# One-core transformer stack: forgetting attention with shared row terms, two banks per step and divided probabilities

## Chip, core and metric

The kernel runs on one core of one Trainium2 chip. The metric is the device time of one execution in microseconds (us). PE is TensorE's matmul row, PEld its weight loads, DVE is VectorE, ACT is ScalarE, POOL is GpSimd.

## Reference, cut to what matters

Three layers run over 256 tokens of width 1024. The change lies in the third, in one of its three mixers, "forgetting attention" (fox): eight heads of width 64, softmax over earlier tokens, with a bias made of summed log gates.

```python
def _fox_mixer(q, k, v, f_logit, f_bias, q_g, k_g):
    ...
    log_f = jax.nn.log_sigmoid(f_logit.astype(jnp.float32) + f_bias.astype(jnp.float32))
    Fc = jnp.cumsum(log_f, axis=1).transpose(0, 2, 1)
    ...
    for blk in range(T // Q_BLOCK):                       # Q_BLOCK = 128
        lo, hi = blk * Q_BLOCK, (blk + 1) * Q_BLOCK
        s = (jnp.einsum('bhqd,bhkd->bhqk', qh[:, :, lo:hi], kh[:, :, :hi]) * scale
             + Fc[:, :, lo:hi, None] - Fc[:, :, None, :hi])
        mask = (lo + jnp.arange(Q_BLOCK))[:, None] >= jnp.arange(hi)[None, :]
        p = jax.nn.softmax(jnp.where(mask, s, -jnp.inf), axis=-1)
        outs.append(jnp.einsum('bhqk,bhkd->bhqd', p, vh[:, :, :hi]))
```

The term of the query's own row, `Fc[t]`, is the same for a whole row of the softmax and drops out; the kernel adds only the row `-Fc[s]`.

## The kernel before

The program writes TensorE's work in one stream. Projections (`prod`, lines 238 to 242, and `project_T`, lines 303 to 305) are the main stream; they multiply split float32r operands, with weights that arrive by DMA as `raw` and are split by ACT (`hi`, line 209) and DVE (`lo`, line 210). Norms and attention are side chains: generators that put their own products between those of the projections and yield an estimate of the microseconds that the other engines need before the chain goes on. A scheduler then orders each engine's instructions; each engine runs its own list in that order.

`fox(h)` is such a chain, for half h of the tokens (128 queries; h = 0 sees 128 keys, h = 1 sees 256). It is run for h = 0 and then for h = 1, woven into the projections of the values (line 1512) and of the first gate. `scores(q)` fills one PSUM bank: four heads for h = 0, two for h = 1. Per head it adds the row of summed gates (two products of an 8-row one-hot column with the rows' high and low parts `fs`, line 1278), the product of queries and keys (a float32 product of 64 rows, line 1284, recorded at the helper's line 363), and the mask (line 1288). Then come the negated maximum (DVE, line 1291) and an exponential per head with its sum (ACT, line 1294). `values` transposes the probabilities (line 329), copies them to SBUF (DVE, line 1302), and multiplies them, as the stationary operand of 128x128, with the values of 64 columns (line 1305, recorded at 363). At the end one DVE product divides all heads by their sums (line 1322), and four more transposes and `fill` make the split operand `yb` of the branch's projection, which comes much later in the stream.

Stick-breaking attention of the second layer (line 961 on) has products of the same forms elsewhere in this kernel: `zbanks` puts 64-row products of even and odd heads into two banks by turns, and its last loop holds the values stationary (64 columns) and writes heads to the lower and upper 64 partitions of one bank.

Of the kernel before, what the change touches and what calls it, by code (L numbers as in the profile page):

```python
# [13 lines left out]
P = 128  # L14
# [38 lines left out]
class Net:  # L53
    """Two halves of 128 tokens run skewed through the whole chain (nothing in the first half
    depends on the second), so that one half's products cover the other's dependent steps.
    Every projection holds the transposed activations stationary and streams the weights; both
    operands are split exactly into a float32r part and the float32r remainder, and three
    products carry each term.

    The program is traced in the order of the tensor engine's work: `steps` are the projections;  # L60
    norms and attention are side chains (generators that yield the microseconds their other
    engines need before the tensor engine's next part), woven in between a projection's products.
    """

    LEAD = 14.85  # how far ahead of its use a weight chunk is split
    LEAD_DMA = 24.0
    WARM = 5, 3, 2  # products of zeros in the gaps before the first projection

    def __init__(self, tc, ins, out, ctx, stop=99):
# [12 lines left out]
        self.now = 0.0  # the tensor engine's clock, by the count of its work  # L82
        self.main = 0.0  # the projections' share of it
# [3 lines left out]
        self.wplan = []  # (time of use, weight piece)  # L87
        self.plan = 0.0

# [33 lines left out]
    def get(self, slot):  # L123
        """waits for a slot in the projections' stream."""
# [32 lines left out]
    def weight(self, ap, r0, nk, c0, ncol, us=None):  # L157
        """plans a weight chunk for the steps planned next; its k tiles appear in ["hl"]."""
# [54 lines left out]
    def fetch(self, out, ap, late=False):  # L213
        """late: not ahead of the loads that are traced before."""
# [1184 lines left out]
    def second(self, x, xT, mk, mv, nxt):  # L1399
# [60 lines left out]
        def use_d(h, i, ps, r):  # L1460
            if i == 0:
                fsp[h] = self.fox_gate(ps[:, :8], r)
                if h == 1:
                    self.spawn(self.fox_rows(fsp, sl["fr"]))
# [256 lines left out]
```

## Time and profile before

| what | value |
|---|---|
| median of 3 runs | 1351.44 us (1350.68 to 1352.32) |
| span of the profiled execution, first to last instruction | 1349.8 us |
| PE busy | 1331.2 us (99%) |
| PEld busy | 1195.6 us (89%) |
| DVE busy | 811.7 us (60%) |
| ACT busy | 693.2 us (51%) |
| DMA read from HBM | 222.03 MB, 165 GB/s over the span |
| mean granted clock of TensorE | 0.992 |

The profiled execution's span is 1.6 us under the median; what lies around it (start and end of the program) is in the runs' times alone. PE's row counts a matmul until its modelled end, and consecutive matmuls overlap, so the time that a product really takes of the stream is the distance from its start to the next one's. A granted clock of 1.00 is 2.4 GHz, 0.50 is 1.2 GHz.

### The profile page before, as it was taken

The numbers are of one execution on the slowest core, as the hardware profiler recorded it, in microseconds if no ns is written. First come the engines' busy times: TensorE is split into PE (matmuls) and PEld (weight loads), VectorE is DVE, ScalarE is ACT, GpSimd is POOL, SyncE is SP. The second block draws the span as 40 slices with busy tenths as digits, with TensorE's granted clock in tenths as the row PEclk, the third lists the DMA queues.
The fourth block names the chain that finished last, engine by engine and source line by source line (L and its number), as shares of the span: only waits on it lengthen the run. The fifth ranks groups of instructions, "written<-read, shape, count | busy, mean of one in ns | idle before, by whom it ended". The sixth has DMA issues, their size and how long they took to land.

```text
span 1349.8 us, 21557 instructions
## 1 busy us (share of the span) xinstructions
PE 1331.2 (99%) x8506; PEld 1195.6 (89%) x8509; DVE 811.7 (60%) x1208; ACT 693.2 (51%) x1128; POOL 126.9 (9%) x224
## 2 busy tenths in 40 slices
PE   8999999999999999999999999998999999999998
PEld 5899888899998999888889999897987999899997
DVE  6665576644447565477664444767774456766552
ACT  6855555643437576574564344754443344645441
POOL 3000001000001000017100000114142020000000
PEclk9999999999999999999999999999997999999999
DMA  7854553646554643464464655463352346465551
GB/s 244 296 183 138 173 190 102 219 160 203 187 187 160 222 136 120 140 229 123 148 200 161 204 185 188 142 192 112 96 155 82 107 127 216 142 203 174 188 183 34
DMA packets 121439, 224.48 MB, mean 166 GB/s; under 512 B 7448, under 2 KB 19066, under 8 KB 121338
## 3 DMA queue, kind: packets, MB, share of 16 engines
q1 hardware_dynamic: 121338, 223.11, 51.5%
q8 instruction: 67, 1.10, 0.3%
q14 instruction: 34, 0.28, 0.1%
HBM read 222.03 MB, written 1.05 MB: 165 GB/s over the span
## 4 chain that ended last, share of the span: by engine, by line
PE 88%; DVE 4%; issue 3%; POOL 3%; ACT 2%; DMA 0%; DVEq 0%; ACTq 0%; POOLq 0%
PE mm L242 12%; PE mm L239 12%; PE mm L238 12%; PE tr L305 8%; PE tr L304 8%; PE tr L303 8%; PE tr L363 5%; PE mm L303 5%; PE mm L304 5%; PE mm L305 5%; PE tr L329 3%; PE tr L242 1%; PE tr L239 1%; PE tr L238 1%; DVE lo L210 1%
## 5 line engine op out<-in xcount | busy, mean ns | idle before, releaser
L210 DVE TENSOR_TENSOR lo<-raw,hi 128x1024 fp32r<-128x1024 f32 (+1 forms) x414 | 496.9, 1224 | 268.6 <-ACT hi L209 262.1
L209 ACT CAST hi<-raw 128x1024 fp32r<-128x1024 f32 (+1 forms) x414 | 419.7, 1042 | 221.2 <-PE mm L242 98.4
L238 PE MATMUL mm<-hi,t 128*128 128x512 f32 (+2 forms) x856 | 330.7, 388 | 0.0
L239 PE MATMUL mm<-lo,t 128*128 128x512 f32 (+2 forms) x856 | 328.4, 385 | 0.3 <-DVE lo L210 0.3
L242 PE MATMUL mm<-hi,t 128*128 128x512 f32 (+2 forms) x856 | 268.0, 388 | 0.0
L303 PE MATMUL tr<-t,hi 128*128 128x256 f32 x864 | 244.7, 283 | 0.0
L305 PE MATMUL tr<-t,lo 128*128 128x256 f32 x864 | 244.5, 283 | 0.0
L304 PE MATMUL tr<-t,hi 128*128 128x256 f32 x864 | 244.5, 283 | 0.0
L239 PEld LDWEIGHTS mm<-lo,t 128*128 128x128 f32 x856 | 162.1, 189 | 30.7 <-DVE lo L210 0.7
L238 PEld LDWEIGHTS mm<-hi,t 128*128 128x128 f32 x856 | 162.1, 189 | 29.0
L242 PEld LDWEIGHTS mm<-hi,t 128*128 128x128 f32 x856 | 159.7, 189 | 30.7 <-issue 0.4
L303 PE MATMUL mm<-t,hi 128*128 128x256 f32 x576 | 166.8, 290 | 0.0
L304 PEld LDWEIGHTS tr<-t,hi 128*128 128x128 f32 x864 | 165.8, 192 | 0.6
L303 PEld LDWEIGHTS tr<-t,hi 128*128 128x128 f32 x864 | 165.8, 192 | 0.6
L305 PEld LDWEIGHTS tr<-t,lo 128*128 128x128 f32 x864 | 165.8, 192 | 0.0
L305 PE MATMUL mm<-t,lo 128*128 128x256 f32 x576 | 163.7, 284 | 0.0
L304 PE MATMUL mm<-t,hi 128*128 128x256 f32 x576 | 163.7, 284 | 0.0
L303 PEld LDWEIGHTS mm<-t,hi 128*128 128x128 f32 x576 | 111.0, 193 | 1.6 <-issue 0.3
L304 PEld LDWEIGHTS mm<-t,hi 128*128 128x128 f32 x576 | 111.0, 193 | 0.8
L305 PEld LDWEIGHTS mm<-t,lo 128*128 128x128 f32 x576 | 110.9, 192 | 0.0
L375 POOL TENSOR_SCALAR s<-s 128x1 f32<-128x1 f32 x32 | 23.2, 725 | 798.0 <-ACT junk L381 786.8
L363 PE MATMUL tr<-t,t 128*128 128x128 f32 (+4 forms) x672 | 89.7, 297 | 4.1 <-DVE t L1155 3.4
(240 smaller groups left out, 1218.0 us busy)
## 6 DMA issues: line engine op xcount, KB each, us to landing
raw<-in_ffn_w_gate_up SPq DMA_DIRECT2D x88, 512.0 KB
raw<-in_ffn_w_down SPq DMA_DIRECT2D x66, 512.0 KB
raw<-in_w_in SPq DMA_DIRECT2D x54, 512.0 KB
raw<-in_ffn_w_up SPq DMA_DIRECT2D x44, 512.0 KB
raw<-in_xa_w_kv SPq DMA_DIRECT2D x32, 512.0 KB
raw<-in_sb_w_qkv SPq DMA_DIRECT2D x24, 512.0 KB
raw<-in_ml_w_in SPq DMA_DIRECT2D x22, 512.0 KB
raw<-in_xa_w_q SPq DMA_DIRECT2D x16, 512.0 KB
```

The costliest lines, as they stand in the source:

```text
L209: self.nc.scalar.copy(hi, raw)
L210: self.nc.vector.tensor_sub(lo, raw, hi.bitcast(F32))
L238: nc.tensor.matmul(out, lhsT=a, rhs=wh, start=first and k == 0, stop=False)
L239: nc.tensor.matmul(out, lhsT=a, rhs=wl, start=False, stop=False)
L242: nc.tensor.matmul(out, lhsT=b, rhs=hl[k][0], start=False, stop=last and k == nk - 1)
L303: self.nc.tensor.matmul(out, lhsT=wh, rhs=xh, start=k == 0, stop=False)
L304: self.nc.tensor.matmul(out, lhsT=wh, rhs=xl, start=False, stop=False)
L305: self.nc.tensor.matmul(out, lhsT=wl, rhs=xh, start=False, stop=k == kt - 1)
L329: self.nc.tensor.transpose(ps[:, i * P : (i + 1) * P], src(i), self.ident)
L363: self.nc.tensor.matmul(out, lhsT=lhsT, rhs=rhs, start=start, stop=stop, **kw)
L375: nc.gpsimd.tensor_scalar(e, a, EPS, b, ALU.add, ALU.add)
```

## The change

The row of summed gates becomes one product per head with 128 rows: the gates' sums are kept in one tile `f` of 128 partitions, the high part on rows 0 to 7 and the remainder on rows 32 to 39, zeros elsewhere, and `sel` selects both of a head's rows. A call of `scores` fills two banks, even heads in one and odd heads in the other: first one mask product for all heads of a bank, then the row terms, then the query-key products, which alternate between the banks. Sums are inverted per bank and each head's probabilities are divided on DVE before they are transposed. The values are the stationary operand (64 columns), the transposed probabilities stream (128 columns), and even and odd heads write the lower and the upper 64 partitions of `o`, which is then already the transposed result: the closing product and the closing transposes go. Yields in the chain are 6.0 and 2.4 where they were 1.5, 1.4 and 1.0.

```diff
-    def fox_gate(self, ps, r):
+    def fox_gate(self, ps, r, sp):
...
-        nc.vector.tensor_add(sp, a, e)
-        return sp
+        for c in (0, 32):
+            nc.vector.tensor_add(sp[:, c : c + 8], a, e)
...
-        mm(ps[:8, 0:128], lhsT=sp[0], rhs=self.up, start=True, stop=True)
-        mm(ps[:8, 128:256], lhsT=sp[1], rhs=self.up, start=True, stop=False)
-        mm(ps[:8, 128:256], lhsT=sp[0], rhs=self.onesf, start=False, stop=True)
-        fh, fl = self.t2([8, 256], F32R), self.t2([8, 256], F32R)
-        nc.vector.tensor_copy(fh, ps[:8, :256])
-        nc.vector.tensor_sub(fl, ps[:8, :256], fh.bitcast(F32))
-        slot.v = (fh, fl)
+        mm(ps[:, 0:128], lhsT=sp[:, 0, :], rhs=self.up, start=True, stop=True)
+        mm(ps[:, 128:256], lhsT=sp[:, 1, :], rhs=self.up, start=True, stop=False)
+        mm(ps[:, 128:256], lhsT=sp[:, 0, :], rhs=self.onesf, start=False, stop=True)
+        f = self.t2([P, 256], F32R)
+        nc.vector.tensor_copy(f, ps[:, :256])
+        nc.vector.tensor_sub(f[32:40], ps[32:40, :256], f[32:40].bitcast(F32))
+        slot.v = f
...
-        # even and odd heads in banks of their own
-        def scores(q):
...
+        def scores(g):
+            banks = [self.bank(), self.bank()]
+            vs = [b.rearrange("p (k s) -> p k s", k=per) for b in banks]
+            for v in vs:
+                nc.tensor.matmul(
+                    v[:, :, h * P :], lhsT=self.identb, rhs=self.m_nat[:, :per, :], start=True, stop=False, **kw
+                )
+            self.pe(MM * per / 2)
+            for i in range(per):
+                for q in range(2):
+                    hd = 2 * per * g + 2 * i + q
+                    nc.tensor.matmul(
+                        vs[q][:, i, :], lhsT=self.sel[:, hd : hd + 1].to_broadcast([P, P]), rhs=fr[:, : n * P],
+                        start=False, stop=False, **kw,
+                    )
+                    self.pe(MM * n / 4)
+            for i in range(per):
+                k = per * g + i
                 for s in range(n):
-                    self.mmf(
-                        v[:, i, s * P : s * P + P], sl["fq", h].v[r, hd // 2, :], sl["fk", s].v[r, hd // 2, :],
-                        False, s < h, **kw,
+                    for q in range(2):
+                        r = slice(q * 64, q * 64 + 64)
+                        self.mmf(
+                            vs[q][:, i, s * P : s * P + P], sl["fq", h].v[r, k, :], sl["fk", s].v[r, k, :],
+                            False, True, **kw,
+                        )
+            res = []
+            for v in vs:
+                mx, sm, rc = [self.small(per) for _ in range(3)]
+                nc.vector.tensor_reduce(mx, v, axis=AX.X, op=ALU.max, negate=True)
+                p = self.t2([P, per, n * P])
+                for i in range(per):
+                    nc.scalar.activation(
+                        p[:, i, :], v[:, i, :], AF.Exp, bias=mx[:, i : i + 1], accum_out=sm[:, i : i + 1]
+                    )
+                nc.vector.reciprocal(rc, sm)
+                for i in range(per):
+                    nc.vector.tensor_scalar(p[:, i, :], p[:, i, :], rc[:, i : i + 1], None, ALU.mult)
+                res.append(p)
+            return res
...
+            yield 2.4
+            for i in range(per):
+                k = per * g + i
                 for s in range(n):
-                    self.mmf(
-                        o[:, hd * 64 : hd * 64 + 64], pT[:, i, s, :], sl["fv", s].v[:, hd * 64 : hd * 64 + 64],
-                        s == 0, s == n - 1,
-                    )
+                    for q in range(2):
+                        hd = 2 * k + q
+                        self.mmf(
+                            o[q * 64 : q * 64 + 64, k * P : k * P + P], sl["fv", s].v[:, hd * 64 : hd * 64 + 64],
+                            pT[q][:, i, s, :], s == 0, s == n - 1, **kw,
+                        )
...
-        nc.vector.reciprocal(rc, sm)
-        t = self.t2()
-        nc.vector.tensor_mul(
-            t.rearrange("p (k t) -> p k t", k=8), o.rearrange("p (k t) -> p k t", k=8),
-            rc.unsqueeze(2).to_broadcast([P, 8, 64]),
-        )
-        yield 1.0
-        self.fill(self.transpose4(lambda i: t[:, i * P : (i + 1) * P]), y, h)
+        self.fill(o, y, h)
...
-        self.id8 = self.const([8, 8], F32R, "id8")
-        nc.vector.tensor_copy(self.id8, self.ident[:8, :8])
+        self.sel = self.const([P, 8], F32R, "sel")
+        nc.vector.tensor_add(self.sel, self.ident[:, 0:8], self.ident[:, 32:40])
+        self.fsp = self.const([P, 2, P], F32, "fsp")
+        nc.vector.memset(self.fsp, 0.0)
```

The order of instructions shows how the scheduler places this. First PE, at the first scores of half 0 in the program before: `tr_10614` is the bank of the scores, `t_9430` and `t_9431` the rows' high and low parts, `t_10569` and `t_10416` queries and keys.

```order
L1278 MATMUL tr_10614<-t_9430,id_5901 128x128
L1278 MATMUL tr_10614<-t_9431,id_5901 128x128
L363 MATMUL tr_10614<-t_10569,t_10416 128x128
L1288 LDWEIGHTS identb
L1288 MATMUL tr_10614<-m_nat,identb 128x128
L1278 MATMUL tr_10614<-t_9430,id_5901 128x128
```

The same place on PE in the changed program; two banks, `tr_10612` and `tr_10613`, and one tile of row terms, `t_9432`.

```order
L1277 LDWEIGHTS identb
L1277 MATMUL tr_10612<-m_nat,identb 128x512
L1277 LDWEIGHTS identb
L1277 MATMUL tr_10613<-m_nat,identb 128x512
L1284 MATMUL tr_10612<-t_9432,sel 128x128
L1284 MATMUL tr_10613<-t_9432,sel 128x128
...
L363 MATMUL tr_10612<-t_10570,t_10417 128x128
L363 MATMUL tr_10613<-t_10570,t_10417 128x128
```

Before, each head's three kinds of product follow one another, eight times in two blocks with six projection products between the blocks; now two masks, eight row terms and eight query-key products stand in one block.

Next DVE of the changed program, right behind that block: `s_10632` and `s_10646` are the two banks' maxima, `t_10636` and `t_10650` their probabilities.

```order
L1301 TENSOR_REDUCE s_10632<-tr_10612 128x4
L1307 RECIPROCAL s_10634<-s_10633 128x4
L1301 TENSOR_REDUCE s_10646<-tr_10613 128x4
L1309 TENSOR_SCALAR t_10636<-t_10636,s_10634 128x128 x4
L356 COPY t_10665<-tr_10660 128x512
L210 TENSOR_TENSOR lo_10680<-raw_10534,hi_10679 128x1024
L1307 RECIPROCAL s_10648<-s_10647 128x4
L210 TENSOR_TENSOR lo_10687<-raw_10537,hi_10686 128x1024
L1309 TENSOR_SCALAR t_10650<-t_10650,s_10648 128x128 x4
L1318 COPY t_10722<-tr_10717 128x512
```

The second bank's division stands behind a copy and two weight splits; before, a bank's only DVE work between scores and transposes was its maximum. Last, PE of the changed program where these probabilities are transposed.

```order
L305 MATMUL mm_10704<-t_8721,lo_10474 128x256
L329 MATMUL tr_10717<-ident,t_10636 128x128 x4
L303 MATMUL mm_10704<-t_8748,hi_10484 128x256
L304 MATMUL mm_10704<-t_8749,hi_10484 128x256
L329 MATMUL tr_10724<-ident,t_10650 128x128
L305 MATMUL mm_10704<-t_8748,lo_10485 128x256
L329 MATMUL tr_10724<-ident,t_10650 128x128
L303 MATMUL mm_10704<-t_8748,hi_10484 128x256
L329 MATMUL tr_10724<-ident,t_10650 128x128 x2
```

The second bank's four transposes come right behind the first bank's, with four products of the projection among them.

## Rows read from the trace of the kernel before

**Rows 1.** The page: busy time of PE, and one costly group.

```profile
PE 1331.2 (99%) x8506; PEld 1195.6 (89%) x8509; DVE 811.7 (60%) x1208; ACT 693.2 (51%) x1128; POOL 126.9 (9%) x224
...
L239 PE MATMUL mm<-lo,t 128*128 128x512 f32 (+2 forms) x856 | 328.4, 385 | 0.3 <-DVE lo L210 0.3
```

**Rows 2.** Windows: length, busy us of PE, PEld, DVE, ACT, POOL; then granted clock.

```profile
1026.27:1031.24 4.97, 4.27 (x22) 3.08 (x21) 1.74 (x4) 0.00 (x0) 0.00 (x0) 0.87 0.19 71
1029.90:1043.56 13.66, 13.66 (x42) 9.99 (x42) 3.88 (x5) 4.20 (x15) 0.00 (x0) 0.50 0.13 40
1034.93:1041.00 6.07, 6.07 (x22) 4.35 (x21) 0.00 (x0) 0.00 (x0) 0.00 (x0) 0.50 0.29 86
1053.45:1055.79 2.34, 2.34 (x16) 1.76 (x15) 0.76 (x2) 0.65 (x2) 0.00 (x0) 1.00 0.01 4
1067.46:1070.86 3.40, 3.40 (x18) 3.40 (x18) 1.92 (x2) 2.59 (x7) 0.00 (x0) 0.50 0.74 274
929.00:933.00 4.00, 1.56 (x13) 1.39 (x13) 3.47 (x11) 0.00 (x0) 1.83 (x4) 1.00 0.46 131
466.50:469.75 3.25, 3.09 (x39) 2.33 (x39) 2.37 (x3) 2.43 (x5) 0.00 (x0) 1.00 0.84 250
```

**Rows 3.** Timeline of PE, first scores of half 0: start, length, instruction [idle before].

```profile
1027.40 0.48 PE L363 MATMUL tr<-t,t 64*128 64x128 f32 x2 [0.70 <-DVE t L356]
...
1027.98 0.43 PE L1278 MATMUL tr<-t,id 8*128 8x128 f32 x2
...
1028.92 0.43 PE L1278 MATMUL tr<-t,id 8*128 8x128 f32 x2
```

**Rows 4.** Timeline of PE in stick-breaking attention: 64-row products by turns, masks, values.

```profile
468.40 1.16 PE L363 MATMUL tr<-t,t 64*128 64x128 f32 x16
469.49 0.61 PE L533 MATMUL tr<-m_lt,identb 128*128 128x512 bf16 x2
...
483.37 2.19 PE L363 MATMUL tr<-t,t 128*64 128x128 f32 x32
485.49 0.38 PE L303 MATMUL mm<-t,hi 128*128 128x256 f32 x1
```

**Rows 5.** Timeline of PE: fox's value products, and the last closing transposes.

```profile
1045.23 0.62 PE L242 MATMUL mm<-hi,t 128*128 128x512 f32 x2
1045.69 0.28 PE L303 MATMUL mm<-t,hi 128*128 128x256 f32 x1
1045.81 0.28 PE L304 MATMUL mm<-t,hi 128*128 128x256 f32 x1
...
1046.04 1.00 PE L363 MATMUL o<-t,t 128*128 128x64 f32 x8
...
1047.05 0.28 PE L304 MATMUL mm<-t,hi 128*128 128x256 f32 x1
...
1087.33 0.60 PE L329 MATMUL tr<-ident,t 128*128 128x128 f32 x4
...
1087.88 0.28 PE L304 MATMUL mm<-t,hi 128*128 128x256 f32 x1
```

**Rows 6.** Groups by form on DVE: busy us, mean ns of one, idle before.

```profile
L210 DVE TENSOR_TENSOR lo<-raw,hi 128x1024 fp32r<-128x1024 f32 x406 | 491.0, 1233 | 264.7 <-ACT hi L209 258.2
...
L356 DVE COPY t<-tr 128x512 f32<-128x512 f32 x10 | 6.8, 684 | 1.0 <-PE tr L329 1.0
...
L943 DVE TENSOR_SCALAR t<-t,cols 128x128 f32<-128x128 f32 x8 | 2.4, 345 | 0.0
...
L1291 DVE TENSOR_REDUCE s<-tr 128x4 f32<-128x512 f32 x2 | 1.4, 692 | 10.1 <-PE tr L1288 10.1
```

**Rows 7.** Timeline of ACT: first exponential and last sum of one bank.

```profile
1033.00 0.36 ACT L1294 ACTIVATE t<-tr,s 128x128 f32<-128x128 f32 x1
...
1034.29 0.21 ACT L1294 ACTIVATION_READ_ACCUMULATOR t<-tr,s 128x1 f32 x1
```

**Rows 8.** Timeline of PE: its longest wait for DVE in the third layer.

```profile
931.79 0.41 PE L363 MATMUL tr<-t,t 128*128 128x64 f32 x2 [2.44 <-DVE t L1155]
```

More of the change, by code (lines that the diff above doesn't have):

```diff
@@ L1230, in chain_head @@
         slot.v = self.to_T(t, None if scale is None else self.foxg[:, scale : scale + 1])
-    def fox_gate(self, ps, r):
+    def fox_gate(self, ps, r, sp):
         nc = self.nc
-        z, a, e, sp = [self.small(8) for _ in range(4)]
+        z, a, e = [self.small(8) for _ in range(3)]
         nc.vector.scalar_tensor_tensor(z, ps, r, self.fox_bias, ALU.mult, ALU.add)
@@ L1264, in fox @@
         yield from self.until(sl["fr"], sl["fq", h], *[sl[k, s] for k in ("fk", "fv") for s in range(n)])
-        fs = sl["fr"].v
+        fr = sl["fr"].v
         o = self.psm.tile([P, 512], F32, tag="mm", name=self.name("o"))
-        sm, mx, rc = self.small(8), self.small(8), self.small(8)
-        def scores(q):
-            heads = [q // 2 * 2 * per + 2 * i + q % 2 for i in range(per)]
-            r = slice(q % 2 * 64, q % 2 * 64 + 64)
-            ps = self.bank()
-            v = ps.rearrange("p (k s) -> p k s", k=per)
-            kw = dict(skip_group_check=True)
-            for i, hd in enumerate(heads):
-                for j, f in enumerate(fs):
+        kw = dict(skip_group_check=True)
@@ L1280, in scores @@
-                        start=j == 0, stop=False, **kw,
+                        vs[q][:, i, :], lhsT=self.sel[:, hd : hd + 1].to_broadcast([P, P]), rhs=fr[:, : n * P],
+                        start=False, stop=False, **kw,
                     )
                     self.pe(MM * n / 4)
+            for i in range(per):
+                k = per * g + i
                 for s in range(n):
-                    self.mmf(
-                        v[:, i, s * P : s * P + P], sl["fq", h].v[r, hd // 2, :], sl["fk", s].v[r, hd // 2, :],
-                        False, s < h, **kw,
-                    )
@@ L1288, in scores @@
-                nc.tensor.matmul(
-                    v[:, i, h * P :], lhsT=self.identb, rhs=self.m_nat[:, 0, :], start=False, stop=True, **kw
-                )
-            nc.vector.tensor_reduce(mx[:, heads[0] : heads[-1] + 1 : 2], v, axis=AX.X, op=ALU.max, negate=True)
-            p = self.t2([P, per, n * P])
-            for i, hd in enumerate(heads):
-                nc.scalar.activation(
-                    p[:, i, :], v[:, i, :], AF.Exp, bias=mx[:, hd : hd + 1], accum_out=sm[:, hd : hd + 1]
-                )
@@ L1297, in scores @@
-            return heads, p
-        def values(heads, p):
-            tp = self.transpose4(lambda j: p[:, j // n, j % n * P : j % n * P + P])
-            pT = self.t2([P, per, n, P])
-            nc.vector.tensor_copy(pT, tp.rearrange("p (k s t) -> p k s t", k=per, s=n))
-            yield 1.4
-            for i, hd in enumerate(heads):
-                for s in range(n):
-                    self.mmf(
-                        o[:, hd * 64 : hd * 64 + 64], pT[:, i, s, :], sl["fv", s].v[:, hd * 64 : hd * 64 + 64],
-                        s == 0, s == n - 1,
-                    )
+                    for q in range(2):
[4 more added lines that the diff above has]
+                        )
@@ new lines, in scores, with values @@
+            return res
+        def values(g, ps):
+            pT = []
+            for p in ps:
+                tp = self.transpose4(lambda j: p[:, j // n, j % n * P : j % n * P + P])
+                t = self.t2([P, per, n, P])
+                nc.vector.tensor_copy(t, tp.rearrange("p (k s t) -> p k s t", k=per, s=n))
+                pT.append(t)
+            yield 2.4
+            for i in range(per):
+                k = per * g + i
+                for s in range(n):
+                    for q in range(2):
[4 more added lines that the diff above has]
+                        )
@@ L1311, in fox @@
         prev = None
-        for q in range(8 // per):
-            cur = scores(q)
-            yield 1.5
+        for g in range(n):
+            cur = g, scores(g)
+            yield 6.0
             if prev is not None:
@@ L1406, in second @@
         ya, yb, yc = (Halves(2) for _ in range(3))
-        gates, merged, fsp = {}, {}, {}
+        gates, merged = {}, {}
         def chain_f(h, ps, r):
@@ L1461, in use_d @@
             if i == 0:
-                fsp[h] = self.fox_gate(ps[:, :8], r)
+                self.fox_gate(ps[:, :8], r, self.fsp[:, h, :])
                 if h == 1:
-                    self.spawn(self.fox_rows(fsp, sl["fr"]))
+                    self.spawn(self.fox_rows(self.fsp, sl["fr"]))
                 ps = ps[:, 8:]
```

3 lines of the change are left out of this document (removed).

## The prediction

> **What bounds the kernel.** I read the page first: PE is busy for 99% of the span [rows 1], so time is won where PE's stream gets shorter and lost where PE has to wait. The reader should not take "busy" for "fast", though: the next view, the windows over fox's stretch, shows it. From 1029.90 to 1043.56 and again from 1067.46 to 1070.86 the granted clock is 0.50, the 1.2 GHz level, while PE counts as busy all the time [rows 2]. Fox's PE work lies between 1026.27 (its first scores) and 1087.88 (behind its last transposes), woven into projections that are there in either kernel; at both ends of the program PE's order is the same but for about a hundred instructions near 920 us that shift a little. So the question is how long that stretch becomes.
>
> What did PE do before the clock fell? From 1026.27 on it ran the first scores: products of 8 rows, of 64 rows and small masks, one wait of 0.70 us for a copy on DVE [rows 3], busy for 4.27 of 4.97 us [rows 2]. At 1067.46 again a block of scores had just ended. Stick-breaking's block of 64-row products, which fill both halves of the array by turns [rows 4], passed at 1.00, with TensorE busy for 3.09 of 3.25 us (466.50 to 469.75, [rows 2]).
>
> The Trainium skill (TensorE: Matmul & The Clock Gate, "Why this matters for your kernels") warns of idle gaps of PE between bursts as what brings the half clock. The trace differs here: the longest wait ahead of the fall is 0.70 us, while a wait of 2.44 us at 931.79 left the clock at 1.00. By that rule alone the low-clock term below would not exist in the kernel before; the rows show that it does, so it is counted.
>
> **What goes.**
> (a) The score blocks. Half 0 has two, 4.97 and 6.07 us [rows 2]; one head takes 0.94 us at full clock (1027.98 to 1028.92, [rows 3]), more at half. Half 1 has four blocks of 2.34 us [rows 2], one row for all four. Together 4.97 + 6.07 + 9.36 = 20.4 us.
> (b) Projection products that ran at half clock outside these blocks: 1031.24 to 1034.93, 1041.00 to 1043.56 and 1067.46 to 1070.86, 9.65 us, of which half, 4.8 us, is lost to the clock.
> (c) Six batches of value products: from 1046.04 to 1047.05, less one projection product of 0.12, makes 0.89 us [rows 5]; six are 5.3 us.
> (d) Two batches of closing transposes: 1087.33 to 1087.88 less 0.12, 0.43 us each [rows 5], 0.9 us.
> Sum: 31.4 us. The wait of 0.70 us is in (a): in the new order masks and row terms stand ahead of the first query-key product, and cover that copy.
>
> **What comes.**
> (e) Scores of half 0: two masks of 512 columns at no more than 0.31 each (0.61 for two), eight row terms, eight query-key products by turns, 1.09 us (468.40 to 469.49) [rows 4], and 0.1 for the change of form. The row term with 128 rows is nowhere in the trace. Bounds: 0.10 us, a record with the same weight size and 64 columns (0.81 us for eight, [rows 5]), and 0.18, half the 0.36 that two 8-row ones took. I take 0.12, the step of a full-array float32r product with its own weights (1045.69 to 1045.81, [rows 5]), nearest in form. 0.6 + 1.0 + 1.1 + 0.1 = 2.8 us.
> (f) Half 1, two blocks: masks 0.6 at most (half the columns), four row terms 0.5, products 1.1, change 0.1: 2.3 us each, 4.6 us.
> (g) Value products, three batches of eight: 483.37 to 485.49 holds eight such products and then eight query-key products [rows 4], so 2.12 - 1.09 = 1.03, and 0.1 for the change of form; 3.4 us. The probabilities' 24 transposes are in both kernels.
> (h) A wait in half 0. DVE runs in order, and its list behind the scores is: maximum 0.69, (ACT: four exponentials, 1.50, 1033.00 to 1034.50 [rows 7]), second maximum 0.69, four divisions at 0.30 (2.4 us for eight, the nearest form), a copy 0.68, two splits of 1.23, four divisions [rows 6]. The first head of the second bank is divided 0.69 + 1.50 + 0.69 + 1.2 + 0.68 + 2.46 + 0.30 = 7.5 us after the scores, with hand-overs some 8; the last some 9. PE's own work up to that transpose, by the order: four transposes 0.43, 19 projection products at 0.23 (1045.23 to 1045.69 for two) 4.4, twelve at 0.12, 1.4, four transposes 0.43, two products 0.24: 6.9 us. So PE waits about 1 us here. Below: 0, if ACT and DVE overlap better; above: 3, if one more split of 1.23 and its cast come in front. I take 1.0. Behind that wait stand the value products and the scores of half 1, which move with it. In half 1 at least 57 projection products (6.8 us) and the next block lie between scores and transposes, against a chain of about 6 us: nothing.
> Sum: 2.8 + 4.6 + 3.4 + 1.0 = 11.8 us.
>
> At nothing I take: 16 divisions and four more reciprocals on DVE (5 us, less the two closing products), hidden since DVE is busy for 60% [rows 1] and PE waited for its splits for 0.3 us in all [rows 1]; without that cover they cost the delay of each split behind them. The gates' tile of 128 rows near 920 us (one more small DVE addition, three products of unchanged columns): its place shifts by a few products among waits of PE; at most 1 us either way. DMA: projections pass faster here; behind 1067.46 it moved 274 GB/s with PE never waiting [rows 2].
>
> **Sum.** 31.4 - 11.8 = 19.6 us off a span of 1349.8, that is 1330.2; the runs' median lies 1.6 us over the span: **1331.8 us**.
>
> **Rivals.**
> *The clock still falls.* The block of half 0 with the transposes and the wait behind it is still lighter than a projection. For it: the fall at 1067.46 came after a block of only 2.34 us. Against: row terms use 128 rows now, query-key products fill both halves as in stick-breaking, which held 1.00 (466.50 to 469.75); and the 2.44 us wait [rows 8] left the clock at 1.00 [rows 2]. One more stretch of 3.4 us at half clock costs 1.7 us (1333.5); if as much stays low as before (17.06 us), 8.5: 1340.
> *The other engines become the bound of the chain.* The division puts DVE, ACT and DVE again between scores and transposes, per bank. If each of the three groups makes PE wait 2 to 3 us, 1336 to 1338. Against: the 57 products of half 1. The Trainium skill (TensorEngine Tiling (Array Packing), "PSUM Bottleneck") says that packing speeds up TensorE but not what reads PSUM behind it, which is this rival; its price here is the one of the rows just given, and no run yet shows it.
> *The halves don't run side by side.* Then products by turns take twice as long: 3 blocks and 3 batches, about 6 us: 1338. Against: [rows 4] shows the same forms doing so.
> *Slower.* Weight splits stand behind divisions in DVE's list; where a split comes late, PE stops in its projection. To end above 1354, these waits would have to reach 22 us in a stretch of some 43: each of about ten splits 2 us late. PE's 0.3 us of such waits in the whole program [rows 1] speaks against it. The price up to that point is just a smaller gain.
>
> **Numbers.** Forecast as summed 0.72 (1328.5 to 1335: row terms and masks at their lower bounds and no wait take off 2 us and the stretch near 920 us one more; the wait's upper bound and one low-clock stretch add 3.7); clock 0.12; chain 0.10; not side by side 0.02; slower 0.02; no change 0.02. To leave out no more than 2 in 10 on the high side, where the rivals lie, the range goes to 1338. About 0.2%, 2.7 us, is what a measurement of this kernel can tell from no change: faster 0.96, same 0.02, slower 0.02.
>
> **What would show it.** Granted clock 1.00 from 1026 to 1070; the first scores one block of about 2.8 us, those of half 1 of about 2.3; value batches of 1.1; a wait of PE of about 1 us before the second bank's transposes in half 0, and none in half 1; 19 to 20 us between the ends of fox at the same projection product. It is wrong if windows at 0.50 remain, if query-key pairs start 0.2 us apart in place of together, or if PE's projection products begin to wait for `lo`.

## Result and profile after

| | before | after |
|---|---|---|
| median, lowest to highest, of 4 runs each | 1351.88 us (1350.68 to 1353.94) | 1330.69 us (1330.33 to 1331.52) |
| span of the profiled execution | 1349.8 us | 1328.9 us |

The ratio is 0.9843, 95% interval 0.9829 to 0.9856: faster by 1.6%. The forecast was 1331.8 us.

The page of the changed kernel, as in [rows 1]: PE's share of the span has not moved, and its wait for `lo` at line 239 went from 0.3 us to none.

```profile
PE 1311.2 (99%) x8475; PEld 1180.9 (89%) x8475; DVE 814.7 (61%) x1229; ACT 693.1 (52%) x1128; POOL 125.2 (9%) x224
...
L239 PE MATMUL mm<-lo,t 128*128 128x512 f32 (+2 forms) x856 | 327.6, 384 | 0.0
```

To see where 20.9 us of span went, I take the same two projection products in either trace, one shortly before fox's first scores and one behind its last transposes, and measure between their weight loads. This is that stretch in the kernel before (columns as in [rows 2]; the number ahead of the last two columns is the granted clock):

```profile
1020.69:1094.12 73.43, 72.73 (x466) 63.86 (x464) 31.49 (x41) 24.32 (x57) 4.57 (x5) 0.88 0.33 101
```

and in the changed kernel the same stretch, then the scores of half 0, a batch of value products and a score block of half 1:

```profile
1021.23:1073.04 51.81, 51.70 (x431) 47.80 (x430) 33.68 (x59) 24.21 (x57) 4.57 (x5) 1.00 0.47 149
...
1026.72:1029.19 2.47, 2.47 (x28) 2.14 (x27) 1.82 (x4) 0.00 (x0) 0.00 (x0) 1.00 0.39 144
1039.59:1040.62 1.03, 1.03 (x18) 0.86 (x17) 0.71 (x1) 0.00 (x0) 0.00 (x0) 1.00 0.65 159
1040.62:1042.50 1.88, 1.88 (x24) 1.62 (x23) 0.76 (x2) 0.65 (x2) 0.00 (x0) 1.00 0.93 302
```

The stretch is 73.43 - 51.81 = 21.62 us shorter, and the clock in it is 1.00 where it was 0.88. It begins 0.54 us later than before (1021.23 against 1020.69); that leaves 21.1 us, and some 0.2 are given back behind it.

PE's timeline of the changed kernel at the first scores answers to [rows 3]; the next rows show the transposes of the two banks, where the prediction put a wait:

```profile
1026.72 0.60 PE L1277 MATMUL tr<-m_nat,identb 128*128 128x512 bf16 x2
1026.97 1.19 PE L1284 MATMUL tr<-t,sel 128*128 128x128 f32 x8
1028.10 1.16 PE L363 MATMUL tr<-t,t 64*128 64x128 f32 x16
1029.19 0.66 PE L329 MATMUL tr<-ident,t 128*128 128x128 f32 x4
...
1035.45 0.60 PE L329 MATMUL tr<-ident,t 128*128 128x128 f32 x4
...
1036.01 0.28 PE L304 MATMUL mm<-t,hi 128*128 128x256 f32 x1
1036.40 0.30 PE L329 MATMUL tr<-ident,t 128*128 128x128 f32 x1
```

The reader is to see start-to-start times: two masks 0.25 us, eight row terms 1.13, eight query-key products 1.09, nothing between them. The sixteen records of the query-key products, merged in this row, start in pairs of an even and an odd head, 0.01 us apart within a pair, so the halves do run together. The projection product of 1036.01 ends at 1036.29, by its modelled end, and the second bank's first transpose starts at 1036.40: a wait of 0.11 us. Counted from start to start, as the prediction counts, that product takes 0.12 us and the wait is 0.27. DVE's timeline behind these scores shows why it is so short:

```profile
1032.22 0.86 DVE L1309 TENSOR_SCALAR t<-t,s 128x128 f32<-128x128 f32 x4
1033.00 0.68 DVE L356 COPY t<-tr 128x512 f32<-128x512 f32 x1
1033.61 1.22 DVE L210 TENSOR_TENSOR lo<-raw,hi 128x1024 fp32r<-128x1024 f32 x1
1034.74 0.17 DVE L1307 RECIPROCAL s<-s 128x4 f32<-128x4 f32 x1
1034.83 1.23 DVE L210 TENSOR_TENSOR lo<-raw,hi 128x1024 fp32r<-128x1024 f32 x1
1035.97 0.87 DVE L1309 TENSOR_SCALAR t<-t,s 128x128 f32<-128x128 f32 x4
```

Four divisions take 0.78 us from the first to the copy behind them (1032.22 to 1033.00), where 1.2 was counted; copy and splits follow as forecast.

### The profile page after: what moved, and what is told of

The parts are those of the page before. It is cut to its first block, busy times and chain, and to the rows that moved or that the text cites. A ratio compares the mean times of both kernels' runs of the same rounds, so it can differ in the third digit from the quotient of the medians.

```text
span 1328.9 us, 21515 instructions
## 1 busy us (share of the span) xinstructions
PE 1311.2 (99%) x8475; PEld 1180.9 (89%) x8475; DVE 814.7 (61%) x1229; ACT 693.1 (52%) x1128; POOL 125.2 (9%) x224
## 4 chain that ended last, share of the span: by engine, by line
PE 78%; issue 14%; DVE 2%; POOL 2%; ACT 2%; DMA 1%; SPq 0%; DVEq 0%; POOLq 0%; ACTq 0%
PE mm L242 11%; PE mm L239 11%; PE mm L238 11%; PE tr L305 8%; PE tr L304 8%; PE tr L303 8%; PE tr L363 4%; PE mm L303 3%; PE mm L304 3%; PE mm L305 3%; PE tr L329 3%; PE tr L242 2%; PE tr L239 2%; PE tr L238 2%; DVE lo L210 1%
## 5 line engine op out<-in xcount | busy, mean ns | idle before, releaser
L363 PE MATMUL tr<-t,t 128*128 128x128 f32 (+4 forms) x672 | 82.1, 292 | 2.9 <-DVE t L1155 2.9
```

The lines of the kernel that those rows point to most:

```text
L363: self.nc.tensor.matmul(out, lhsT=lhsT, rhs=rhs, start=start, stop=stop, **kw)
```

## Experiments

Two questions were put. What had lowered the clock? And what is each form worth at full clock? Every kernel was profiled and timed in 4 runs or more beside runs of the kernel before on the same chip. The stretch is the one between the same two products; "at 0.50" is what of it ran at the low clock in the profiled execution; the clocks are the means over each whole execution, for all timed runs.

| kernel | median us | ratio to before, 95% interval | stretch us | at 0.50, us | clocks |
|---|---|---|---|---|---|
| before | 1351.88 | | 73.43 | 17.06 | 0.989 to 0.996 |
| after | 1330.69 | 0.9829 to 0.9856 | 51.81 | 0 | 0.996 to 0.999 |
| e4: before, 128-row term | 1340.92 | 0.9907 to 0.9940 | 62.18 | 0 | 0.996 to 0.999 |
| e6: before, no row term | 1342.06 | 0.9911 to 0.9944 | 61.82 | 3.42 | 0.993 to 0.997 |
| e10: before, one 8-row term | 1348.73 | 0.9961 to 0.9982 | 67.40 | 6.82 | 0.989 to 0.996 |
| e9: before, both terms | 1354.05 | 1.0006 to 1.0031 | 76.98 | 20.49 | 0.987 to 0.994 |
| e12: before, by kind | 1339.10 | 0.9884 to 0.9936 | 61.00 | 0 | 0.997 to 0.999 |
| e1: after, 8-row terms | 1333.86 | 0.985 to 0.988 | 54.28 | 0 | 0.995 to 0.996 |
| e7: e1 head by head | 1345.53 | 0.9941 to 0.9970 | 66.10 | 10.24 | 0.992 to 0.994 |
| e2: after, no turns | 1332.38 | 0.9841 to 0.9871 | 53.34 | 0 | 0.996 to 1.000 |
| e3: after, values as before | 1333.08 | 0.9846 to 0.9876 | 54.48 | 0 | 0.996 to 1.000 |
| e8: the same, head by head | 1333.70 | 0.9853 to 0.9883 | 54.48 | 0 | 0.996 to 0.998 |
| e5: after, old yields | 1332.92 | 0.9844 to 0.9877 | 53.66 | 0 | 0.996 to 0.999 |
| e11: after, no row terms | 1329.64 | 0.982 to 0.985 | 50.77 | 0 | 0.996 to 0.999 |

What the 17.06 us at 0.50 cost is a little less than half of them. These rows of PE's timeline before lie in the first window:

```profile
1033.52 0.63 PE L238 MATMUL mm<-hi,t 128*128 128x512 f32 x1
1033.94 0.63 PE L239 MATMUL mm<-lo,t 128*128 128x512 f32 x1
...
1034.93 0.69 PE L1278 MATMUL tr<-t,id 8*128 8x128 f32 x2
...
1036.49 0.69 PE L1278 MATMUL tr<-t,id 8*128 8x128 f32 x2
```

A projection product takes 0.42 us here and 0.23 at full clock [rows 5], a head of scores 1.56 us and 0.94 [rows 3]. The next table adds up each stretch from the start of one product to the start of the next, by what the products do:

| kernel | 280 projection products, us | scores, us | transposes, us | values, us |
|---|---|---|---|---|
| before | 43.85 | 20.36 | 4.11 | 5.11 |
| e12 | 39.75 | 12.70 | 3.63 | 4.92 |
| after | 39.53 | 6.23 | 2.98 | 3.08 |

Projections and transposes are the same in the kernel before and in e12, which kept 1.00, and took 4.6 us less there. In the scores, four heads of the second bank took 6.07 us in place of 3.8, and the last head of the first 1.4 in place of 0.9. So I estimate the clock at 7.4 us, and the stretch before at full clock at 66.0.

The profiled executions of e1 to e3, e5 to e9 and, for a shorter time, e12 have a low-clock window near 930 us, outside the stretch; it is told of at the end. In e1 the part from one earlier projection product to the stretch (895.04 to 1021.03) is 125.99 us long, and the same part takes 124.98 in the changed kernel, so about 1 us between these two executions is not the edit. The stretch is what I compare.

### The clock

**e4_before_row128.** The kernel before, with only the row term changed (with the gates' tile and `sel`, as in the change); everything else stays head by head, one bank at a time.

```diff
...
-                for j, f in enumerate(fs):
-                    nc.tensor.matmul(
-                        v[:, i, :], lhsT=self.id8[:, hd : hd + 1].to_broadcast([8, P]), rhs=f[:, : n * P],
-                        start=j == 0, stop=False, **kw,
-                    )
+                nc.tensor.matmul(
+                    v[:, i, :], lhsT=self.sel[:, hd : hd + 1].to_broadcast([P, P]), rhs=fs[:, : n * P],
+                    start=True, stop=False, **kw,
+                )
...
```

> The kernel before (1351.9 us) with the row term alone changed: one product of 128 rows per head in place of two of 8; one bank per step, heads one behind the other, mask last, closing division and transposes stay. Theory L: the 8-row products are gone, the clock stays at 1.00 or falls for one stretch; the two blocks of half 0 then take about 3.2 us each in place of 4.97 and 6.07, projections lose nothing to the clock (4.8), half 1 saves 0.2 per head: 1340 to 1342 us. Theory W: the wait of 0.7 us shrinks little and the changes of form stay, so the clock falls as before, for 13 us or so: 16 products fewer save 2 to 4 us, 1348 to 1350 us.

Its stretch, and PE's timeline at the first head:

```profile
1021.27:1083.45 62.18, 61.18 (x450) 55.56 (x449) 31.55 (x41) 24.18 (x57) 4.56 (x5) 1.00 0.39 119
```

```profile
1027.97 0.48 PE L363 MATMUL tr<-t,t 64*128 64x128 f32 x2 [1.00 <-DVE t L356]
...
1028.66 0.48 PE L363 MATMUL tr<-t,t 64*128 64x128 f32 x2
```

The clock stays at 1.00 although the wait ahead of the scores is 1.00 us, longer than the 0.70 of [rows 3], and although the changes of form are still there. So neither the wait nor the changes of form alone had lowered it; the time, 1340.92 us, is theory L's. Of the 11.25 us that this one edit gives, about 7.4 are the clock by the estimate above. The Trainium skill (TensorE: Matmul & The Clock Gate, "Why this matters for your kernels") names idle gaps between bursts as what brings the half clock; these rows don't show it, since of these two kernels the one with the longer gap kept its clock.

**e1_rows8 and e7_rows8_head_by_head.** The changed kernel with the 8-row terms back: in e1 all of a block's row terms stand together and its query-key products follow by turns; in e7 each head's query-key products stand right behind its row terms. This is e1's diff, without the gates' tile, which is as before again:

```diff
...
-                    nc.tensor.matmul(
-                        vs[q][:, i, :], lhsT=self.sel[:, hd : hd + 1].to_broadcast([P, P]), rhs=fr[:, : n * P],
-                        start=False, stop=False, **kw,
-                    )
+                    for f in fr:
+                        nc.tensor.matmul(
+                            vs[q][:, i, :], lhsT=self.id8[:, hd : hd + 1].to_broadcast([8, P]), rhs=f[:, : n * P],
+                            start=False, stop=False, **kw,
+                        )
...
```

> The changed kernel (1330.7 us) with the row terms as they were: two products of 8 rows per head in place of one of 128 rows, everything else kept (two banks, masks first, query-key products by turns). Theory L (the clock fell because the products before it filled few rows): 16 products of 8 rows stand behind one another in half 0 for some 2 us and 8 in each block of half 1, so stretches at granted clock 0.50 come back; row terms cost 1.2 us more per block (16 at 0.13 against 8 at 0.11), 3.6 in all, and one to three low stretches of 3.4 us cost 1.7 each: 1336 to 1339 us. Theory W (the clock fell because of the 0.70 us wait and the changes of form from head to head): neither is here, the clock stays at 1.00 and only the extra products cost: 1334 us.

> The changed kernel with two 8-row row terms per head as in the kernel before and each head's query-key products right behind them (masks still one per bank, heads still alternate between the banks head by head, divided probabilities and stationary values stay). Theory R (8-row products mixed head by head with 64-row ones lower the clock; in one block of their own they do not): a window at 0.50 starts within about 4 us of the scores of half 0 at 1027, and the time is 1331 plus 2.3 for the 8-row terms, 1.7 for products not by turns and 3 to 8 for the clock: 1338 to 1343. Theory B (it took the whole pattern of before, masks per head, two blocks with projections between them and a wait): clock 1.00, 1334.5 to 1336.

The windows of e1 and of e7 (for e7 the stretch and its two low windows, and in PE's timeline its wait ahead of the first query-key product):

```profile
1021.03:1075.31 54.28, 53.99 (x447) 49.52 (x446) 33.75 (x59) 24.14 (x57) 4.57 (x5) 1.00 0.46 145
895.04:1021.03 125.99, 121.10 (x880) 115.01 (x879) 92.19 (x200) 58.47 (x107) 40.16 (x49) 0.97 0.40 121
```

```profile
1022.07:1088.17 66.10, 65.68 (x446) 57.68 (x446) 33.96 (x59) 24.64 (x57) 4.57 (x5) 0.92 0.39 116
1033.26:1040.09 6.83, 6.83 (x21) 5.36 (x22) 4.05 (x10) 4.25 (x18) 0.00 (x0) 0.50 0.00 0
1053.74:1057.15 3.41, 3.41 (x18) 3.41 (x17) 2.06 (x7) 2.11 (x8) 0.00 (x0) 0.50 0.00 0
```

```profile
1028.80 0.49 PE L363 MATMUL tr<-t,t 64*128 64x128 f32 x2 [0.28 <-DVE t L356]
```

e1 missed theory L: sixteen 8-row products in a row left the clock at 1.00 and cost only their time, 2.47 us in the stretch, so L as I had put it (8-row products are too light, wherever they stand) fell. The time is theory W's, which had missed e4: neither theory held in both kernels. e7 has e1's products in another order and loses 11.8 us more, some 4.2 of them to the clock (2.6 in projections, 0.6 in transposes, 1.0 in two heads at 0.50). Theory R was right on the fall, though it came 5.7 us behind the first mask (1027.56) and not within 4; its sum, up to 1343, was too low, because the alternation itself cost more than I had counted.

**e12_before_by_kind.** The kernel before with the same products, one bank at a time, in another order within a bank.

```diff
-            for i, hd in enumerate(heads):
-                for j, f in enumerate(fs):
-                    nc.tensor.matmul(
...
-                for s in range(n):
-                    self.mmf(
...
-                nc.tensor.matmul(
-                    v[:, i, h * P :], lhsT=self.identb, rhs=self.m_nat[:, 0, :], start=False, stop=True, **kw
-                )
+            for i, hd in enumerate(heads):
+                nc.tensor.matmul(
+                    v[:, i, h * P :], lhsT=self.identb, rhs=self.m_nat[:, 0, :], start=i == 0, stop=False, **kw
+                )
...
+            for i, hd in enumerate(heads):
+                for f in fs:
+                    nc.tensor.matmul(
...
+            for i, hd in enumerate(heads):
+                for s in range(n):
+                    self.mmf(
```

> The kernel before with nothing changed but the order within a bank's scores: first the masks of its heads, then all their 8-row products, then all their query-key products, in place of head by head (one bank at a time, the same products, the same two blocks in half 0). Theory O (it is the alternation of narrow products of different forms, head by head, that lowers the clock, as between the two orders of 8-row terms in the changed kernel): no window at 0.50 in fox's stretch, or one of 3.4 us; and fewer changes of form shorten the blocks, half 0 from 3.8 to about 2.2 us per bank, half 1 from 2.34 to about 1.6: 1352 less 8.5 for the clock less 6 for the blocks is 1337 to 1340. Theory B (narrow products lower the clock in any order): 10 us or more at 0.50 stay, 1343 to 1346.

Its stretch, and PE's timeline at the first bank and at one of half 1:

```profile
1020.66:1081.66 61.00, 61.00 (x465) 56.68 (x464) 31.51 (x41) 24.22 (x57) 4.57 (x5) 1.00 0.40 122
```

```profile
1026.15 0.40 PE L1277 MATMUL tr<-m_nat,identb 128*128 128x128 bf16 x4
1026.48 1.10 PE L1283 MATMUL tr<-t,id 8*128 8x128 f32 x8
1027.51 1.16 PE L363 MATMUL tr<-t,t 64*128 64x128 f32 x8
1028.59 0.50 PE L242 MATMUL mm<-hi,t 128*128 128x512 f32 x1
...
1054.98 0.28 PE L1277 MATMUL tr<-m_nat,identb 128*128 128x128 bf16 x2
...
1056.93 0.39 PE L303 MATMUL mm<-t,hi 128*128 128x256 f32 x1
```

Theory O was right. The order alone gives 12.43 us: about 7.4 by the clock, and 5.0 because the blocks are shorter at full clock too. A bank of half 0 takes 2.44 us (1026.15 to 1028.59), that is 0.61 per head, where a head took 0.94 in [rows 3]; a bank of half 1 takes 1.95 (1054.98 to 1056.93), where it took 2.34 [rows 2]. There is no wait for the copy either, since masks and row terms now stand ahead of the first query-key product. That the wait went is not what kept the clock: e4 kept it with a wait of 1.00 us, and e7 lost it with one of 0.28.

**e6_before_no_row_terms, e10_before_one_8row_term, e9_before_both_terms.** How much of it is the 8-row products? The kernel before, head by head, without them (the gates' bias is missing), with one in place of two (the remainder is missing), and with both kinds.

```diff
-                for j, f in enumerate(fs):
+                for j, f in enumerate(fs[:1]):
```

That is e10; e6 drops the loop, and e9 puts a 128-row product, each side carrying half of the term, ahead of it.

> The kernel before with the row of summed gates left out of the scores (its two 8-row products per head are gone; the gates' bias is missing from the softmax); 64-row products and masks stay head by head, one bank per step. Theory R (the 8-row products among the others are what lowers the clock; 64-row products one after another and the same changes of form do not): clock 1.00 through all of fox, as with the 128-row term, and the time of that kernel, 1340.9, less 16 row terms of 0.11 to 0.2 us: 1337.5 to 1339.5. Theory N (the blocks are too light whatever is narrow in them; the 128-row terms only made up for it): windows at 0.50 remain in fox's stretch, 5 us or more lost, 1343 to 1348.

> The kernel before with one 8-row product per head in place of two (the remainder of the row of summed gates is left out of the scores). Between the kernel before, two such products with 17.1 us at 0.50 in fox's stretch, and the one with none, 3.4 us at 0.50. Theory A (a matter of degree): something between, 3.4 to 13.7 us at 0.50: 1351.8 less 2.2 for the products less 1.7 to 6.8 for the clock, 1343 to 1348. Theory B (8-row products bring it, however many): about 17 us at 0.50, 1349.5.

> The kernel before with half of the row term by its two 8-row products per head, and the other half by one 128-row product ahead of them: every product of before is there, and sixteen more. By the runs so far two 8-row products take 2.3 us more in all than one of 128 rows, which itself takes some 2.2 us for the sixteen. Theory A (what counts is how much of the array the block as a whole uses; products of all rows in between make up for narrow ones): clock 1.00 in fox's stretch or one short window at 0.50, 1340.9 + 4.5 = 1345.4, up to 1347, faster than the kernel before although it does more. Theory B (8-row products between 64-row ones bring the half clock by themselves): windows at 0.50 of 10 us and more, 1351.8 + 2.2 = 1354.

The wait ahead of e6's first scores in PE's timeline, then the low windows of e6, of e10 and of e9 inside the stretch:

```profile
1029.17 0.48 PE L363 MATMUL tr<-t,t 64*128 64x128 f32 x2 [1.14 <-DVE t L356]
```

```profile
1030.87:1034.29 3.42, 3.42 (x12) 2.79 (x12) 1.63 (x3) 1.80 (x6) 0.00 (x0) 0.50 0.00 0
```

```profile
1030.11:1033.52 3.41, 3.41 (x11) 2.50 (x11) 1.76 (x2) 2.15 (x8) 0.00 (x0) 0.50 0.00 0
1036.94:1040.35 3.41, 3.41 (x11) 2.42 (x11) 1.92 (x2) 2.33 (x9) 0.00 (x0) 0.50 0.00 0
```

```profile
1034.22:1051.29 17.07, 17.07 (x55) 13.11 (x55) 4.96 (x6) 5.95 (x19) 0.00 (x0) 0.50 0.14 37
1075.18:1078.60 3.42, 3.42 (x18) 3.42 (x18) 1.91 (x2) 3.04 (x7) 0.00 (x0) 0.50 0.57 214
```

Without any 8-row product (e6), 3.42 us stay at 0.50, between theories R (none) and N (5 us or more lost): 64-row products and masks, head by head, can lose some clock without them. A wait of 1.14 us, the longest ahead of any of these scores, stands before them; what share it has is not shown. With one (e10) the profiled execution shows 6.82 us, but that was the fastest of ten (1345.69 us at a mean clock of 0.996). Its median of 1348.73 us lies between what the two theories gave, and its clocks (0.989 to 0.996) are in the range of the kernel before, so e10 doesn't tell them apart. With both kinds (e9) the profiled execution was the slowest of ten (1359.36 us at 0.987; the fastest took 1352.14 at 0.994), but the median of 1354.05 us is theory B's number: full-array products beside the 8-row ones do not make up for them, and theory A fell.

### The forms at full clock

**e2_one_bank_at_a_time.** The changed kernel, with all of one bank's query-key products ahead of the other's.

```diff
-            for i in range(per):
-                k = per * g + i
-                for s in range(n):
-                    for q in range(2):
+            for q in range(2):
+                for i in range(per):
+                    k = per * g + i
+                    for s in range(n):
```

> The changed kernel with the query-key products bank by bank: four of the even heads, then four of the odd ones, no turns. If turns make two 64-row products run side by side, eight products take about 1.8 us in place of 0.89, in three blocks: +2.7 us, 1333.4. Theory L also allows a low-clock stretch, since half of the rows stand empty for 1.8 us (1335); theory W does not. If turns are worth nothing (the products run one behind the other in either case): 1330.7.

PE's timeline:

```profile
1028.31 1.71 PE L363 MATMUL tr<-t,t 64*128 64x128 f32 x16
1029.95 0.66 PE L329 MATMUL tr<-ident,t 128*128 128x128 f32 x4
```

Eight products take 1.64 us (1028.31 to 1029.95) in place of 1.09 by turns, and the stretch is 1.53 us longer, where 2.7 were expected; that is 0.51 for each of three blocks. By turns they take a third less time, not half. The clock stays at 1.00: turns are not what keeps it up.

**e3_probs_stationary and e8_probs_stationary_by_head.** Values as before. In e3 two heads' products alternate within one bank, and the sums of half 1 mix; in e8 each head's stand together. This is e3's diff:

```diff
-                            o[q * 64 : q * 64 + 64, k * P : k * P + P], sl["fv", s].v[:, hd * 64 : hd * 64 + 64],
-                            pT[q][:, i, s, :], s == 0, s == n - 1, **kw,
+                            o[:, hd * 64 : hd * 64 + 64], pT[q][:, i, s, :], sl["fv", s].v[:, hd * 64 : hd * 64 + 64],
+                            s == 0, s == n - 1, **kw,
...
-        self.fill(o, y, h)
+        t = self.t2()
+        nc.vector.tensor_copy(t, o)
+        yield 1.0
+        self.fill(self.transpose4(lambda i: t[:, i * P : (i + 1) * P]), y, h)
```

> The changed kernel with the value products as they were: transposed probabilities stationary (128x128), 64 columns of values streaming, and the closing copy and four transposes per half. By the prediction's terms (c), (d) and (g): six half-batches of 0.89 against three of 1.03 make +2.2 us, two batches of closing transposes +0.9: 1333.8 us, clock at 1.00 in either theory. If the weight loads of the new form are hidden no better than those of the old one: 1331.5 (the transposes alone).

> The changed kernel with the values as in the kernel before: probabilities stationary, 64 columns stream, a closing copy of the sums and four closing transposes per half; each head's products stand together, so that the sums of half 1 are whole. Term by term: three batches of eight value products with 128-column weights, two product by product 0.89 each per four heads, 1.8 us in place of 1.03 for eight, 2.3 us in three; two batches of closing transposes 0.43 each, 0.9: 3.2 us, 1334. Rival: the closing work falls where PE's stream has slack or the products run closer together than before, 1332 or less.

PE's timeline of e8, one batch of values:

```profile
1040.91 1.90 PE L363 MATMUL o<-t,t 128*128 128x64 f32 x16
1042.62 0.36 PE L303 MATMUL mm<-t,hi 128*128 128x256 f32 x1
```

A batch takes 1.71 us in place of 1.03, three times 0.68, and two closing transposes come back; the stretch is 2.67 us longer in both kernels, where 3.1 and 3.2 were expected. That is what stationary values are worth.

**e11_after_no_row_terms.** The changed kernel without row terms (the gates' bias is missing): the diff only removes the loop of line 1284.

> The changed kernel without row terms (the gates' bias is missing from the softmax): two masks and eight query-key products by turns per block remain. Prices the 128-row terms in their new place: eight at 0.11 us and eight of twice the columns at about 0.18, 2.3 us: 1328.4 if the clock stays at 1.00 (masks of all rows and products by turns are enough). Rival: it is the row terms that keep the clock up, as in the kernel before, where leaving them out gave 3.4 us at 0.50: a window at 0.50 behind one of the three blocks, 1330 or more.

```profile
1026.96 0.60 PE L1277 MATMUL tr<-m_nat,identb 128*128 128x512 bf16 x2
1028.24 1.16 PE L363 MATMUL tr<-t,t 64*128 64x128 f32 x16 [0.67 <-DVE t L356]
1029.33 0.66 PE L329 MATMUL tr<-ident,t 128*128 128x128 f32 x4
```

In PE's timeline of e11 the query-key products wait 0.67 us for the copy on DVE. The stretch is only 1.04 us shorter, where 2.3 were expected. The block of half 0 gives 0.10 of it (2.37 us from 1026.96 to the transposes at 1029.33, in place of 2.47): its row terms were nearly free, since they cover that copy. The two blocks of half 1 give 0.47 each (1.41 in place of 1.88). The rival missed: the clock is 1.00 without them.

**e5_old_yields.** The changed kernel with these two yields as before.

```diff
-            yield 2.4
+            yield 1.4
...
-            yield 6.0
+            yield 1.5
```

> The changed kernel with the chain's yields back at 1.5 us ahead of the values and 1.4 us behind the transposes (6.0 and 2.4 in the changed kernel), all else equal. PE's list then has the first bank's transposes of half 0 after about twelve projection products in place of nineteen and more, and the value products closer behind the copies. Theory D (the divided probabilities put DVE, ACT and DVE into the chain; the long yields are what covers it): PE waits in fox's stretch grow from 0.1 us to 2.5 to 4 us, 1333.5 to 1335, clock 1.00 as waits do not lower it. Theory S (the scheduler finds other work for PE whatever the yields say): 1330 to 1331.5, no wait over 0.3 us. Theory I (waits in this stretch bring the half clock): a window at 0.50 behind the waits, 1337 or more.

```profile
1036.36 0.40 PE L363 MATMUL o<-t,t 128*64 128x128 f32 x2 [0.73 <-DVE t L1318]
```

The stretch is 1.85 us longer, with the wait of 0.73 us for the transposed probabilities shown in this row of PE's timeline, and the clock stays at 1.00. That lies between theories S and D: the division makes the chain longer, and the longer yields are what covers it, but the scheduler hides more than D thought. Of the other 1.1 us, values take 0.8 (the first batch is cut in two, the second takes 1.48 us, 1049.44 to 1050.92, in place of 1.03) and the score block that is woven with them 0.2.

## Why the prediction was right

The time, the sign and the place were right, and the terms came out near their sizes. The span lost 20.9 us where 19.6 were put, because what comes is smaller than forecast; the ends of fox lie 21.1 us apart (1094.12 against 1073.04) where 19 to 20 were named. The ends of the range are rounded: the sums given for them come to 1328.8 and 1335.5, not 1328.5 and 1335.

**What comes** was put at 11.8 us and measured 9.6. (e) 2.8 became 2.47: the masks were taken too high (0.25 in place of 0.6), the row terms a little low (1.13 in place of 1.0). (f) 2.3 per block became 1.88, in the same way: masks 0.15 in place of 0.6, row terms 0.64 in place of 0.5. So the masks are the price most mis-sized, 0.55 us in all where 1.8 was put. (g) 1.13 per batch became 1.03; the 0.1 for the change of form was not there. (h), a wait of 1.0, became 0.27 from start to start. The first bank-two division was put 8 us behind the scores; its transpose starts 7.2 us behind them (1029.19 to 1036.40), mostly because divisions took about 0.2 us apiece and not 0.30. PE's own work took the 6.9 us that were counted. Half 1 has no wait, as said.

**What goes** was put at 31.4. With 9.6 added the stretch should have lost 21.8; it lost 21.6. By the table of sums (a) was 20.36, as put; (b) and (d) together 5.7, as put (4.3 less in projections, which hold the wait of 0.27, and 1.1 less in transposes); (c) 5.1 in place of 5.3. Half of the low time, as (b) and the rivals count it, is somewhat too much: the clock in (a) and (b) is worth about 7.4 us and not 8.5. That it is the clock is shown by e4 and e12, which keep 1.00 and gain 11.25 and 12.43; (c), (d) and (g) together, 2.8 by the prediction, are 2.67 by e8. What (a) and (e) did not name apart is how the blocks' gain splits: the order by kind, 5.0 in e12; 2.47 us for 8-row terms (e1); 1.53 for turns (e2). If these gains add up, 12.4, 2.5, 1.5 and 2.7 leave 2.5 of the 21.6 us that no run took apart, with one mask product per bank and one block in place of two among it.

**Near 920 us** at most 1 us either way was allowed; it cost about 0.3: the part from 896 us to the stretch is 124.98 us long (896.25 to 1021.23), and was 124.65.

**The rivals.** Against the clock's fall the prediction argued that row terms would use 128 rows and query-key products fill both halves. The outcome was right; as the reason it is too narrow. By e12 the same narrow products in one bank at a time, by kind, keep the clock, by e1 8-row terms in one run do so, and by e2 turns are not needed. That the block stands kind by kind is enough; the 128-row term alone was enough too (e4). The chain of DVE and ACT did not become the bound, but with the old yields the stretch is 1.85 us longer, 0.73 of it a wait for this chain (e5). Not side by side would have cost 1.53 us in the score blocks (e2), where the rival put 6 on scores and values together; the values' price by turns was not measured alone.

**Open.** Why alternation head by head lowers the granted clock is not settled. It is not one quantity that I could name: e6 alternates two forms and falls a little, e4 alternates three and does not, and e9, which adds products of all rows to those of before, falls as the kernel before does. Whether one 8-row product per head is better than two stays open as well (e10).

## What to carry to other kernels

Where narrow products of several forms fill one bank, write them kind by kind for all heads and not head by head: here that order alone was worth 12.4 of the 21.6 us, before any form was changed. Read the granted clock of the windows around such a block first, since PE looks busy there at half speed, and compare variants between the same two products of the main stream. A step that is moved into a chain, as the division was, is free only while other work is scheduled into its place.

## What the hardware showed beyond expectation

The order of the same products decided the clock (e1 against e7: 0 against 10.24 us at 0.50 in the stretch).

Changes of form cost time at full clock too. In e12 eight 8-row products take 1.03 us in one run, 0.26 for a pair; in PE's timeline of e7 a pair takes 0.36 (1029.21 to 1029.57), and a pair of records of 64 rows 0.42:

```profile
1029.21 0.43 PE L1285 MATMUL tr<-t,id 8*128 8x128 f32 x2
1029.57 0.48 PE L363 MATMUL tr<-t,t 64*128 64x128 f32 x2
1029.99 0.43 PE L1285 MATMUL tr<-t,id 8*128 8x128 f32 x2
```

Near 930 us, far from fox's scores, e1 ran at 0.50 from 929.90, the end of this wait in PE's timeline, to 936.73:

```profile
929.98 0.66 PE L363 MATMUL tr<-t,t 128*128 128x64 f32 x2 [2.67 <-DVE t L1155]
```

This is the nearest that a run here comes to what the Trainium skill says of idle gaps, named with e4; the wait of 2.44 us at the same place before left 1.00 [rows 8]. So in this kernel a long wait was followed by the half clock in some executions and not in others, and a busy stretch of alternating narrow products was followed by it too. Why one execution lost its clock here and another did not, no run shows.
